# Order of the weight forms S4, S2 and the sum S3 in two up/gate pairs of an encoder step

## The chip, the cores and the metric

The kernel runs on one core of a Trainium2 chip. The metric is the device time of one execution in microseconds. The median of three runs of the kernel before is 1652.66 us (1652.25 to 1654.64).

## The reference, cut to what matters

One inference step of a one-layer encoder: two attention branches in parallel, a gated merge, and then a channel mixer, the part that matters here:

```
def conv_ffn(h, conv_buf, w_upg, conv_w, conv_b, w_down):
    u, g = jnp.split(h @ w_upg, 2, axis=-1)
    s = u.shape[1]
    upad = jnp.concatenate([conv_buf, u], axis=1)
    c = conv_b
    for tap in range(CONV_WIDTH):
        c = c + conv_w[tap] * upad[:, tap:tap + s]
    y = (jax.nn.gelu(c, approximate=True) * g) @ w_down
    return y, upad[:, -(CONV_WIDTH - 1):]
```

`h` has 1152 rows (1024 of a prompt and 8 x 16 of samples) of 1024 channels, in f32; `w_upg` is 1024 x 6144, so u and g have 3072 columns each. Everything is computed to about f32 accuracy.

## The kernel before, in words

**Products.** TensorE multiplies numbers of a shortened format (F32R), so each operand is split into a high part (a copy into F32R, on ScalarE) and a low part (the operand minus the high part, on VectorE or GpSimd). One product is three: high by high, high by low, low by high. A "form" of a weight block is this pair of high and low part, 128 x 512 each; `split` (L1108) makes it, with the copy on L1112 and the subtraction on L1113.

**Seven products instead of eight.** The up/gate stage (about 850 to 1375 us) takes the columns of u and g in 24 blocks of 128. Block f of u and block f of g make a *pair*, and the pair's weights are a 2 x 2 matrix of quarters: q[0, k] of u, q[1, k] of g, with k the half of the 1024 channels. By Winograd's form of Strassen's scheme a pair needs seven products, and each has a weight form and an activation form. In the order in which TensorE does them, with the weight form in brackets: B11 (A11), B21 (A12), B22 (S4), T2 (S2), T4 (A22), T1 of the *next* pair (S1), T3 (S3). The four A forms are quarters as they are. The others are made of sums on VectorE (tiles `s`, a pool of three buffers):

- S1 = q10 + q11 (L1105),
- S2 = S1 − q00, in place over S1 (L1127),
- S4 = q01 − S2 (L1105),
- S3 = q00 − q10 (L1105).

The last of these is the last reader of q00 and q10 in a pair, whose buffers are loaded next with the quarters of the following pair (L1100, on SP's DMA queue).

**Tokens.** The tokens are in two parts of 2 x 320 and 2 x 256 columns. Each product runs for both parts, 12 matmuls each: four channel blocks by (high, high), (high, low), (low, high), so the first two matmuls of a product need only the weight's high part, and the third needs its low part. In the trace a PSUM tile keeps the name of the product that began its sum, so the products read B11 `pa_B`, B21 `pb_B`, B22 `pc_T<-xf_B`, T2 `pa_B<-xf_T`, T4 `pb_T`, T1 `pc_T<-xf_T`, and T3 again `pa_B`, from `xfc` and `xf_T`. Each bank has two buffers, one for each part of the tokens. After a product, `after` (L1185 on) copies or adds its result into the buffers of u and g: ScalarE copies after T1, B11, B22 and T4 (L1191, L1194, L1200, L1205), VectorE adds after B21, T2 and T3 (L1197, L1203, L1207/L1208). B11 of a pair starts a new sum in the bank that T3 of the pair before used, so it needs L1208.

**Also on these engines.** After T2 the convolution of the pair (ScalarE L1228, VectorE L1230, ScalarE's GELU L1232), after T3 the gate's product on GpSimd (L1236), and during B21 the activation forms for the down projection (`z_forms`, L1258 to L1268, VectorE, and DMAs to memory on L1248/L1255). GpSimd also makes the low part of A22 (L1113).

**What sets the order.** Weight forms come out of the generator `weight_forms` in the order of TensorE's products, and the main loop asks for them some steps ahead: `fill` keeps up to three forms ahead, in four slots (`wfb`) used in turn, so a form's first write waits until the product that used its slot four forms earlier has read it. Each engine runs its instructions in one fixed order. That order is drawn up when the program is built: among the instructions that are expected to be ready, the one written first goes first, so an instruction written later overtakes one that isn't ready yet. `tc.keep_in_program_order(ins)` pins an instruction behind the one written just before it on its engine. `held_next` does so while the list `hold_next` isn't empty.

**The two places.** Pairs are numbered by their index in STEPS. Most pairs do both token parts; pairs 0 and 1 do the first part before the rest, pairs 14 and 25 do the second part of the same two blocks. In pair 2 and pair 14 the loop doesn't fill ahead as usual: after T3 (pair 2) or throughout (pair 14) it fills behind the product, and at T1 of the pair that follows (pairs 3 and 15) it doesn't fill at all. So the forms A12 and S4 of pairs 3 and 15 are made only after T3's additions, with `hold_next` set (L1402 to L1405 in the loop), and S2 is asked for at the next step, B11, with `hold_next` empty. The step after that, B21, asks for A22; B22 for S1 of the next pair.

Of the kernel before, what the change touches and what calls it, by code (L numbers as in the profile page):

```python
# [13 lines left out]
AF = mybir.ActivationFunctionType  # L14
ALU = mybir.AluOpType
# [19 lines left out]
NE = 2  # L35
# [9 lines left out]
def fr(ap):  # L45
    return ap.bitcast(F32)
# [3 lines left out]
def encoder_step(ctx, tc, x, w_in, w_o, w_out, w_upg, w_down, kc, vc, state_conv, conv_w, conv_b,  # L50
                 sink, sink_rows, t5t, onehot, relrev, g_pre_mix, g_post_mix, g_pre_ffn, g_post_ffn,
                 y, ka_new, va_new, kb_new, vb_new, conv_new):
    nc = tc.nc
# [864 lines left out]
    v, p = nc.vector, nc.gpsimd  # L918
# [122 lines left out]
    STEPS = [(f, (0,)) for f in range(NE)] + MAIN  # L1041
# [23 lines left out]
    with ExitStack() as ph:  # L1065
# [15 lines left out]
        hold_next = []  # L1081

        def held_next(ins):
            if hold_next:
                tc.keep_in_program_order(ins)
# [4 lines left out]
        def weight_forms():  # L1090

            count = 0
            pairs = {}

            def quarters(i):
                f = STEPS[i][0]
                where = {(0, 0): wqb[0][:, 0], (1, 0): wqb[0][:, 1], (0, 1): wqb[1][:, 0],
                         (1, 1): wqb[1][:, 1] if i % 2 == 0 else wq5[:]}
                for n, k in ((1, 0), (1, 1), (0, 0), (0, 1)):
                    nc.sync.dma_start(where[n, k], w_upg[n * NF + f][:, 4 * k:4 * k + 4])  # L1100
                return where

            def combine(name, a, b, op):
                t = wsp.tile([P, 4, P], F32, name=name, tag="s")
                held_next(v.tensor_tensor(t[:], a, b, op=op))  # L1105
                return t

            def split(src, eng):  # L1108
                nonlocal count
                t = wfb[count // 2 % 2][:, count % 2]  # L1110
                count += 1
                nc.scalar.activation(t[:, 0], src, AF.Copy)  # L1112
                ins = eng.tensor_tensor(t[:, 1], src, fr(t[:, 0]), op=ALU.subtract)  # L1113
                if eng is v:
                    held_next(ins)
                return t

            for i, _, names in ITEMS:
                if i not in pairs:
                    pairs[i] = (quarters(i), {})  # L1120
                q, s = pairs[i]
                for name in names:
                    if name == "S1":
                        s["12"] = combine(f"s1_{i}", q[1, 0], q[1, 1], ALU.add)
                        yield split(s["12"][:], v)
                    elif name == "S4":
                        held_next(v.tensor_tensor(s["12"][:], s["12"][:], q[0, 0], op=ALU.subtract))  # L1127
                        s["4"] = combine(f"s4_{i}", q[0, 1], s["12"][:], ALU.subtract)
                        s["3"] = combine(f"s3_{i}", q[0, 0], q[1, 0], ALU.subtract)
                        yield split(s["4"][:], v)  # L1130
                    elif name == "S2":
                        yield split(s["12"][:], v)
                    elif name == "S3":
                        yield split(s["3"][:], v)
                    else:
                        n, k = int(name[1]) - 1, int(name[2]) - 1
                        yield split(q[n, k], p if name == "A22" and i >= NE else v)
# [208 lines left out]
        dw_ahead, dz_ahead = [], []  # L1346

        forms = weight_forms()
        ahead = [next(forms) for _ in range(2)]
        rest0, rest1 = more_forms(xfp), None  # L1350
# [102 lines left out]
    with p5_stack as ph:  # L1453
        psy = ph.enter_context(tc.tile_pool(name="psy", bufs=1, space=PSUM, reuse_waits="tile"))
        q = ph.enter_context(tc.tile_pool(name="p5b", bufs=1, side="right", reuse_waits="tile"))
# [7 lines left out]
        q = more.enter_context(tc.tile_pool(name="p5c", bufs=1, side="right", reuse_waits="tile"))  # L1463
# [114 lines left out]
        for b in range(NB - 1):  # L1578
# [13 lines left out]
            if first:  # L1592

                z_forms(pr)
                t = act.tile([P, 5, 1024], F32R, name="wf5_56", tag="b0")
                zsf.append(t[:, 4].rearrange("p (a b) -> p a b", a=2))
                down["wf"] += [t[:, i:i + 2].rearrange("p i (a b) -> p i a b", a=2) for i in (0, 2)]
                t = act.tile([P, 3, 1024], F32R, name="wf5_7", tag="b1")
# [187 lines left out]
```

## Time and profile before

| | us |
|---|---|
| Median of three runs | 1652.66 |
| Profiled execution: its time | 1652.35 |
| Profiled execution: first to last instruction (span) | 1650.6 |
| TensorE matmuls busy | 1631.6 (99%) |
| VectorE busy | 1120.4 (68%) |
| ScalarE busy | 776.4 (47%) |
| GpSimd busy | 308.7 (19%) |
| Mean granted TensorE clock | 0.998 |
| One pair in the up/gate stage, TensorE | 22.3 |

In a timeline each row is the start in us, the busy time in us, the engine, the line of the kernel, the operation, what it writes and reads, the number of instructions, and in brackets the idle time of the engine ahead of it with what ended it. PE is TensorE's matmuls, PEld its weight loads, DVE VectorE, ACT ScalarE, POOL GpSimd, SP the engine that issues DMAs. Rows of the same kind that follow each other are merged. `s` are the sums, `wfb` the weight forms, `wqb` and `wq` the quarters as loaded, `wide` the buffers of u, c and g. In a row of stretches, each engine's busy time comes with its number of instructions, in the order PE, PEld, DVE, ACT, POOL.

### The profile page before, as it was taken

Reading aid. Unit: us, or ns where it says so; the run is one execution under the profiler, and the core shown is the slowest. Engines: PE = TensorE matmul, PEld = TensorE weight load, DVE = VectorE, ACT = ScalarE, POOL = GpSimd, SP = SyncE. Lnnn points to the kernel's source line nnn. Section 1 sums busy time; section 2 is a strip of 40 time slices with the busy share of each in tenths; the row PEclk is TensorE's granted clock in tenths of the full one; section 3 lists DMA queues with packets and bytes.
Section 4 is the critical chain, followed back from the end, with each engine's and each line's share of the span. In section 5 each row is a group of like instructions: output and inputs, shape, how many; then the busy total and the mean of one; then the engine's idle time right before and its main releaser. Section 6 shows DMA issues by size and latency. Waiting matters only on the chain.

```text
span 1650.6 us, 28227 instructions
## 1 busy us (share of the span) xinstructions
PE 1631.6 (99%) x10575; PEld 1496.1 (91%) x10575; DVE 1120.4 (68%) x2143; ACT 776.4 (47%) x1627; POOL 308.7 (19%) x308
## 2 busy tenths in 40 slices
PE   9999999999999999999999999999999999999997
PEld 8889889899999998988899999999999998788885
DVE  6355655565555588763488776768777779887797
ACT  5245544444444455436575444444444446433332
POOL 3000000000000000000102222332232223655404
PEclk9999999999999999999999999999999999999999
DMA  5733224232323254752222222223222248444337
GB/s 210 213 88 93 85 86 119 71 104 89 98 89 104 77 165 150 226 187 92 97 71 74 94 93 94 99 94 114 100 97 88 94 149 283 143 147 128 92 112 204
DMA packets 101272, 198.57 MB, mean 120 GB/s; under 512 B 16984, under 2 KB 32904, under 8 KB 101136
## 3 DMA queue, kind: packets, MB, share of 16 engines
q1 hardware_dynamic: 99840, 192.58, 36.7%
q0 software_dynamic: 1008, 3.67, 1.3%
q8 instruction: 83, 1.36, 0.3%
q10 hardware_dynamic: 288, 0.52, 0.1%
q14 instruction: 53, 0.43, 0.1%
HBM read 139.97 MB, written 55.70 MB: 119 GB/s over the span
## 4 chain that ended last, share of the span: by engine, by line
PE 88%; DVE 6%; issue 2%; ACT 1%; POOL 1%; DMA 1%; POOLq 0%; DVEq 0%; SPq 0%; ACTq 0%
PE pa_B L1143 12%; PE pc_T L1143 8%; PE a L1531 5%; PE pb_T L1143 4%; PE pb_B L1143 4%; PE c L1531 2%; PE r L1016 2%; PE r L1015 2%; PE r L1014 2%; PE s L1561 2%; PE o L511 2%; PE o L510 2%; PE pt L467 2%; PE s L442 1%; PE d L1531 1%
## 5 line engine op out<-in xcount | busy, mean ns | idle before, releaser
L1112 ACT ACTIVATE wfb<-s 128x512 fp32r<-128x512 f32 x96 | 60.7, 632 | 132.6 <-PE pa_B L1143 44.7
L1113 DVE TENSOR_TENSOR wfb<-s,wfb 128x512 fp32r<-128x512 f32 x96 | 80.7, 844 | 58.8 <-ACT wfb L1112 57.3
L448 ACT ACTIVATE p<-p,m 128x256 f32<-128x256 f32 (+4 forms) x128 | 76.3, 596 | 83.4 <-DVE m L444 82.1
L1143 PE MATMUL pa_B<-xf_T,wfb 128*128 128x256 f32 (+1 forms) x840 | 114.8, 289 | 0.6 <-DVE wfb L1113 0.6
L1143 PEld LDWEIGHTS pa_B<-xf_T,wfb 128*128 128x128 f32 x840 | 110.7, 188 | 0.8 <-DVE wfb L1113 0.8
L1236 POOL TENSOR_TENSOR wide<-wide 128x512 f32<-128x512 f32 (+1 forms) x46 | 80.8, 1779 | 113.8 <-DVE wide L1208 110.1
L1230 DVE SCALAR_TENSOR_TENSOR wide<-wide,cw 128x640 f32<-128x640 f32 (+2 forms) x140 | 78.9, 606 | 2.7 <-ACT wide L1228 2.6
L1143 PE MATMUL pc_T<-xf_B,wfb 128*128 128x256 f32 (+1 forms) x552 | 77.2, 294 | 1.6 <-DVE wfb L1113 1.6
L1143 PE MATMUL pc_T<-xf_T,wfb 128*128 128x256 f32 (+1 forms) x552 | 76.9, 294 | 0.1
L1143 PE MATMUL pb_T<-xf_T,wfb 128*128 128x256 f32 (+1 forms) x552 | 76.6, 294 | 0.0
L1143 PEld LDWEIGHTS pc_T<-xf_B,wfb 128*128 128x128 f32 x552 | 74.4, 188 | 2.2 <-DVE wfb L1113 2.2
L1143 PEld LDWEIGHTS pc_T<-xf_T,wfb 128*128 128x128 f32 x552 | 74.5, 188 | 0.4 <-DVE wfb L1113 0.4
L1143 PEld LDWEIGHTS pb_T<-xf_T,wfb 128*128 128x128 f32 x552 | 74.4, 188 | 0.0
L1322 POOL TENSOR_TENSOR wf<-wdB,wf 128x1024 fp32r<-128x1024 f32 x23 | 64.4, 2819 | 51.3 <-ACT wf L1321 51.3
L1228 ACT ACTIVATE wide<-wide,cb,cw 128x384 f32<-128x384 f32 (+2 forms) x70 | 46.3, 694 | 38.9 <-DVE wide L1203 38.9
L401 POOL MEMSET bt<- 64x64 f32 x16 | 2.7, 171 | 301.8 <-DMA bt<-ext_b 143.3
L1321 ACT ACTIVATE wf<-wdB 128x1024 fp32r<-128x1024 f32 x36 | 37.0, 1054 | 45.0 <-DVE wdB L1315 32.8
L1531 PE MATMUL a<-wf,z5a 128*128 128x512 f32 x240 | 57.2, 393 | 0.1
L1531 PE MATMUL a<-wf,z5b 128*128 128x512 f32 x240 | 57.0, 393 | 0.0
L1014 PE MATMUL r<-wt,ms 128*128 128x512 f32 x144 | 56.7, 393 | 0.0
L1016 PE MATMUL r<-wt,ms 128*128 128x512 f32 x144 | 56.1, 390 | 0.0
L1015 PE MATMUL r<-wt,ms 128*128 128x512 f32 x144 | 56.1, 389 | 0.0
(677 smaller groups left out, 4896.7 us busy)
## 6 DMA issues: line engine op xcount, KB each, us to landing
wqb<-in_w_upg SPq DMA_DIRECT2D x91, 256.0 KB, 2.7
zf_dr<-wide SPq DMA_DIRECT2D x84, 256.0 KB, 2.2
zr<-zf_dr SPq DMA_DIRECT2D x28, 512.0 KB, 3.8
wdB<-in_w_down SPq DMA_DIRECT2D x48, 256.0 KB, 4.1
z5a<-zf_dr SPq DMA_DIRECT2D x14, 512.0 KB, 3.6
xt<-in_x SPq DMA_DIRECT2D x9, 512.0 KB, 6.7
xr<-in_x SPq DMA_DIRECT2D x9, 512.0 KB, 3.6
x_dr<-xr SPq DMA_DIRECT2D x9, 512.0 KB, 2.6
```

The source lines that it names most:

```text
L448: nc.scalar.activation(p[:, 0:n], p[:, 0:n], AF.Exp, bias=least, scale=-1.0, accum_out=st.d[:, i:i + 1])
L1014: nc.tensor.matmul(ps[:, h], m[:, 0, k], w_rows[k][:, 0, hs], start=k == 0, stop=False)
L1015: nc.tensor.matmul(ps[:, h], m[:, 0, k], w_rows[k][:, 1, hs], start=False, stop=False)
L1016: nc.tensor.matmul(ps[:, h], m[:, 1, k], w_rows[k][:, 0, hs], start=False, stop=k == KD - 1)
L1112: nc.scalar.activation(t[:, 0], src, AF.Copy)
L1113: ins = eng.tensor_tensor(t[:, 1], src, fr(t[:, 0]), op=ALU.subtract)
L1143: nc.tensor.matmul(ps[:, 0:w], wf[:, h, k], xf[:, l, k], start=start and k == 0 and i == 0, stop=stop and k == 3 and i == 2, skip_group_ch ...
L1228: nc.scalar.activation(out, src(0), AF.Identity, bias=cb[:, f:f + 1], scale=cw[:, f, 0:1])
L1230: v.scalar_tensor_tensor(out, src(t), cw[:, f, t:t + 1], out, op0=ALU.mult, op1=ALU.add)
L1236: (v if pr.i < NE else p).tensor_tensor(c, c, pr.g[:, tokens(s)], op=ALU.mult)
L1322: ins = (v if b == 0 or b == NB - 1 or n == 8 else p).tensor_tensor(t[:, 1], src[:], fr(t[:, 0]), op=ALU.subtract)
L1531: nc.tensor.matmul(ps[:], z[:, a, k, t * P:(t + 1) * P], w[:, b, k], start=start and k == 0 and i == 0, stop=k == 1 and i == 2, skip_group ...
```

## The change

For pairs 3 and 15 (`late`: the first pair behind pair NE, and the pair behind one that does a single token part):

- the sum for S3 isn't made between the sum for S4 and S4's low part, but after S2's low part;
- S2's form is made with its ScalarE copy pinned behind the ScalarE instruction written before it (S4's copy), its low part pinned behind the VectorE instruction written before it (S4's low part), and the sum for S3 pinned behind that.

The instructions are the same, and all other pairs are written as before.

```
-            def split(src, eng):
+            def split(src, eng, pinned=False):
                 nonlocal count
                 t = wfb[count // 2 % 2][:, count % 2]
                 count += 1
-                nc.scalar.activation(t[:, 0], src, AF.Copy)
+                ins = nc.scalar.activation(t[:, 0], src, AF.Copy)
+                if pinned:
+                    tc.keep_in_program_order(ins)
                 ins = eng.tensor_tensor(t[:, 1], src, fr(t[:, 0]), op=ALU.subtract)
                 if eng is v:
                     held_next(ins)
@@
                 q, s = pairs[i]
+
+                late = i == NE + 1 or i > NE and len(STEPS[i - 1][1]) == 1
                 for name in names:
@@
                     elif name == "S4":
                         held_next(v.tensor_tensor(s["12"][:], s["12"][:], q[0, 0], op=ALU.subtract))
                         s["4"] = combine(f"s4_{i}", q[0, 1], s["12"][:], ALU.subtract)
-                        s["3"] = combine(f"s3_{i}", q[0, 0], q[1, 0], ALU.subtract)
+                        if not late:
+                            s["3"] = combine(f"s3_{i}", q[0, 0], q[1, 0], ALU.subtract)
                         yield split(s["4"][:], v)
                     elif name == "S2":
-                        yield split(s["12"][:], v)
+                        if late:
+                            hold_next.append(True)
+                        t = split(s["12"][:], v, late)
+                        if late:
+                            s["3"] = combine(f"s3_{i}", q[0, 0], q[1, 0], ALU.subtract)
+                            hold_next.pop()
+                        yield t
```

## The prediction

> **What bounds the kernel now.** I read the page first, for the span and the chain of waits.
>
> ```profile
> span 1650.6 us, 28227 instructions
> PE 88%; DVE 6%; issue 2%; ACT 1%; POOL 1%; DMA 1%; POOLq 0%; DVEq 0%; SPq 0%; ACTq 0%
> ```
>
> TensorE carries 88% of the chain, so only time in which TensorE itself stands still is worth anything. Next I asked who TensorE waited for in the up/gate stage (850 to 1370 us).
>
> ```profile
> PE pc_T L1143 <- DVE wfb L1113: 1.6, 2, 1.0
> ```
>
> Two waits, 1.6 us in all, the longer one 1.0: that is the whole prize. Then the timeline at the first place (pair 3).
>
> ```profile
> 885.36 1.51 PEld L1143 LDWEIGHTS pa_B<-xf_B,wfb 128*128 128x128 f32 x12
> ...
> 887.30 0.68 DVE L1258 TENSOR_TENSOR wide<-wide 128x512 f32<-128x512 f32 x1
> 887.48 0.63 ACT L1112 ACTIVATE wfb<-s 128x512 fp32r<-128x512 f32 x1 [1.34 <-DVE s L1127]
> 887.91 0.68 DVE L1105 TENSOR_TENSOR s<-wqb,s 128x512 f32<-128x512 f32 x1
> 888.01 0.62 ACT L1112 ACTIVATE wfb<-wq 128x512 fp32r<-128x512 f32 x1
> ...
> 888.51 0.68 DVE L1105 TENSOR_TENSOR s<-wqb 128x512 f32<-128x512 f32 x1
> ...
> 888.62 0.63 ACT L1112 ACTIVATE wfb<-s 128x512 fp32r<-128x512 f32 x1
> ...
> 888.71 1.64 POOL L1113 TENSOR_TENSOR wfb<-wq,wfb 128x512 fp32r<-128x512 f32 x1 [1.87 <-ACT wfb L1112]
> ...
> 889.11 2.38 DVE L1113 TENSOR_TENSOR wfb<-s,wfb 128x512 fp32r<-128x512 f32 x2
> ...
> 890.09 0.46 PE L1143 MATMUL pc_T<-xf_B,wfb 128*128 128x320 f32 x2
> ...
> 891.55 3.15 PE L1143 MATMUL pc_T<-xf_B,wfb 128*128 128x320 f32 x22 [1.01 <-DVE wfb L1113]
> ```
>
> ScalarE makes the high part of S2 (887.48), of A22 (888.01), then of S4 (888.62). VectorE makes the sum for S4 (887.91), the sum for S3 (888.51), then two low parts in 2.38 us. The first of the two starts at 889.11, before S4's high part has ended (889.25), so it is S2's, though the code asks for S4's form first. TensorE runs the two matmuls of B22 that need only the high part and stands still for 1.01 us until S4's low part is there (889.11 + 2.38 = 891.49). The first low part alone, from a narrower stretch of the timeline:
>
> ```profile
> 889.11 1.78 DVE L1113 TENSOR_TENSOR wfb<-s,wfb 128x512 fp32r<-128x512 f32 x1
> ```
>
> It takes 1.78 against 0.68 for the sums just ahead of it, and ends 0.54 us after GpSimd's low part of A22 (888.71 + 1.64 = 890.35; 889.11 + 1.78 = 890.89): VectorE waited for GpSimd. The sum of S3, which was already running when GpSimd began, kept its 0.68, and GpSimd then ended 1.16 us after it (889.19). The second place (pair 15), with an ordinary pair's A22 ahead of it:
>
> ```profile
> 1109.96 1.51 PEld L1143 LDWEIGHTS pa_B<-xf_B,wfb 128*128 128x128 f32 x12
> ...
> 1111.64 0.63 ACT L1112 ACTIVATE wfb<-wq 128x512 fp32r<-128x512 f32 x1 [0.91 <-PE pa_B L1143]
> ...
> 1112.36 1.29 POOL L1113 TENSOR_TENSOR wfb<-wq,wfb 128x512 fp32r<-128x512 f32 x1 [0.83 <-ACT wfb L1112]
> ...
> 1142.54 1.51 PEld L1143 LDWEIGHTS pa_B<-xf_B,wfb 128*128 128x128 f32 x12
> ...
> 1144.71 0.68 DVE L1105 TENSOR_TENSOR s<-wqb,s 128x512 f32<-128x512 f32 x1
> ...
> 1145.31 0.68 DVE L1105 TENSOR_TENSOR s<-wqb 128x512 f32<-128x512 f32 x1
> ...
> 1145.51 1.63 POOL L1113 TENSOR_TENSOR wfb<-wq,wfb 128x512 fp32r<-128x512 f32 x1 [1.87 <-ACT wfb L1112]
> ...
> 1147.27 0.46 PE L1143 MATMUL pc_T<-xf_B,wfb 128*128 128x320 f32 x2
> ...
> 1148.34 3.15 PE L1143 MATMUL pc_T<-xf_B,wfb 128*128 128x320 f32 x22 [0.62 <-DVE wfb L1113]
> ```
>
> **The change, part by part.** No instruction is added or removed. In pairs 3 and 15, S2's high part is queued behind S4's on ScalarE, S2's low part behind S4's on VectorE, and S3's sum behind both.
>
> *A22 moves up.* Its form isn't named by the change, but it stood behind S2's high part. It needs the slot of A11, free when B11's weights are loaded: in the ordinary pair it starts 0.17 us after that (1111.47 to 1111.64) and GpSimd 0.72 later. So in pair 3: 886.87 + 0.17 = 887.04, GpSimd asks at 887.76, before the sum for S4. I take it that A22 stays ahead of S4 on ScalarE, as now, since it is ready earlier.
>
> *First place.* GpSimd asks while the subtraction of L1258 runs (to 887.98), so it gets its turn then and ends 1.16 later, 889.14; the sum for S4 ends 0.54 behind it, 889.68 instead of 888.59. S4's high part starts 0.03 after the sum, as now (888.62), so at 889.71. From the start of a high part to that of its low part:
>
> ```profile
> 892.94 0.69 DVE L1105 TENSOR_TENSOR s<-wqb,wqb 128x512 f32<-128x512 f32 x1 [0.71 <-DMA wqb<-in_w_upg]
> 893.75 0.63 ACT L1112 ACTIVATE wfb<-s 128x512 fp32r<-128x512 f32 x1 [4.22 <-DVE s L1105]
> ...
> 894.41 0.69 DVE L1113 TENSOR_TENSOR wfb<-s,wfb 128x512 fp32r<-128x512 f32 x1 [0.78 <-ACT wfb L1112]
> ...
> 894.53 3.34 PE L1143 MATMUL pa_B<-xf_T,wfb 128*128 128x320 f32 x24
> ...
> 900.89 3.34 PE L1143 MATMUL pc_T<-xf_T,wfb 128*128 128x320 f32 x24
> ...
> 905.69 1.51 PEld L1143 LDWEIGHTS pa_B<-xf_T,wfb 128*128 128x128 f32 x12
> ...
> 906.41 0.48 DVE L1207 TENSOR_TENSOR wide<-wide,pa_B 128x320 f32<-128x320 f32 x1
> ...
> 907.40 1.77 PEld L1143 LDWEIGHTS pa_B<-xfa,wfb 128*128 128x128 f32 x12 [0.20 <-issue]
> ```
>
> 0.66 us. S4's low part runs from 890.37 to 891.06, and TensorE resumes 0.06 later, as now, at 891.12 instead of 891.55: 0.43 gained. Bounds: 0 if something else slips in, 1.01 if GpSimd comes after the sum (high part 888.62, low part 889.28 to 889.97, before TensorE asks).
>
> *Second place.* B11's weights are loaded at 1144.05, A22's high part starts at 1144.22, GpSimd asks at 1144.94. The sum for S4 has run since 1144.71 and keeps its 0.68, to 1145.39; GpSimd ends at 1145.39 + 1.16 = 1146.55. S4's high part starts at 1145.42, its low part is held up to 1146.55 + 0.54 = 1147.09, and TensorE wants it at 1147.73. All 0.62 is gained; bounds 0 and 0.62. Together 0.43 + 0.62 = 1.05.
>
> Of the collision, the Trainium skill (SBUF — State Buffer, section Who interferes with whom) says that VectorE instructions with two SBUF inputs and GpSimd instructions that read SBUF exclude each other, the one that starts first holding the ports for its whole instruction. The trace agrees (1.78 against 0.68); the rule speaks against the change, since A22's low part now comes earlier, against the critical sum instead of against S2's low part.
>
> *S2 comes later.* Its low part ends 0.60 behind S4's (the step from 887.91 to 888.51), at 891.66. T2 starts at 894.53 − 0.43; the rest of B22 covers it with 2.4 us, and only past that would it cost.
>
> *S3's sum comes later, and this is what gives time back.* It ends at 892.26 instead of 889.19, 3.07 later; at the second place at 1148.29 instead of 1145.99, 2.30 later. It is the last reader of two quarters, so two of the next pair's four loads move with it on SP's queue (behind them stand only loads for the pair after that; nothing moves on GpSimd's queue but A22's low part):
>
> ```profile
> wqb<-in_w_upg SPq DMA_DIRECT2D x91, 256.0 KB, 2.7
> ```
>
> The sum S1 of the next pair needs one of them. Now it starts 3.75 us after S3's sum ends (892.94 − 889.19), and VectorE is already waiting for it. Three loads were issued together then; the third no longer comes with them, so I put the step at 3.2, between the median load of 2.7 and 3.75. S1's sum then starts 2.5 us later at the first place and 1.75 at the second. T1 is safe: S1's low part would end at 895.10 + 2.5 = 897.6, against 900.46. What is queued behind S1's sum on VectorE is the next pair's other sums, T2's additions, the convolution and at last T3's addition (L1207, 906.41); 0.99 us after that one starts, B11 of the next pair gets its bank (907.40). TensorE already lost 0.20 there. The cover is VectorE's idle time in between:
>
> ```profile
> 892.94:906.41 13.47, 13.47 (x104) 13.47 (x103) 10.76 (x20) 7.93 (x17) 0.98 (x3) 1.00 0.22 69
> 1149.66:1163.07 13.41, 13.41 (x103) 13.41 (x103) 10.75 (x19) 7.96 (x17) 0.91 (x3) 1.00 0.25 71
> ```
>
> The third figure after the length is VectorE's busy time, 10.76 of 13.47 and 10.75 of 13.41, so some 2.7 us stand idle. Not all of it can be filled: 0.78 is the round trip from S1's sum over ScalarE to its low part. But T2's additions and the convolution are written ahead of the next pair's sums, so they can be queued into such gaps. I estimate that 2.4 of it is absorbed; bounds: all of it, and none. First place: 2.5 − 2.4 = 0.1 late, so pair 4's B11 starts 0.1 later than now instead of 0.43 earlier: the gain there is given back. Second place: 1.75 − 2.4 is below zero by 0.65, enough for B11 to keep the 0.62. The rows of TensorE's weight loads there:
>
> ```profile
> 1162.48 1.51 PEld L1143 LDWEIGHTS pa_B<-xf_T,wfb 128*128 128x128 f32 x12
> 1164.07 1.03 PEld L1143 LDWEIGHTS pa_B<-xfa,wfb 128*128 128x128 f32 x7
> ```
>
> B11 began within 0.08 us of T3's last load (1163.99), so this spot too has nothing to spare today.
>
> **The sum.** The profiled execution took 1652.35 us (span 1650.6); that is 0.31 below the median of the runs, 1652.66, and inside their spread (1652.25 to 1654.64). 1652.35 + 0.10 − 0.62 = 1651.83, so 1651.8.
>
> **The rivals.**
>
> *The third sum's delay gets through (slower).* VectorE runs its queue in order; if the queue still has S1's sum ahead of the convolution, it stands in front of a load that lands later, and everything up to T3's addition moves. With half of the idle time absorbed (1.35) and the step at 3.75, pair 4's B11 comes 3.07 − 1.35 = 1.72 later than now and pair 16's 2.30 − 1.35 = 0.95: 1652.35 + 2.67 = 1655.0. With nothing absorbed it is 3.07 + 2.30 = 5.37, 1657.7. With the step at 3.2 it decides the sign from 2.1 us absorbed downwards (2.5 − 2.1 + 1.75 − 2.1 is about nothing). For it: S1's sum waits for its load already now, and L1207 is already the last to arrive. Against it: 2.7 us of idle time, and work written earlier to fill it.
>
> *No collision (faster than I say).* If A22's high part ends up behind S4's on ScalarE, GpSimd begins after the sum for S4, and both waits go whole: 1.01 + 0.62 = 1.63. S3's sum is then 1.09 us earlier at the first place and nothing is given back: 1652.35 − 1.63 = 1650.7. For it: S4's form is written ahead of A22's. Against it: A22 is ready at 887.04, 0.9 us before the sum for S4 can even begin.
>
> *GpSimd first at both places (the change does nothing).* At the second place the sum for S4 leads GpSimd by 0.23 us only (1144.71, 1144.94). If GpSimd leads, it ends at 1144.94 + 1.29 = 1146.23, the sum 0.54 later at 1146.77, S4's high part starts at 1146.80, its low part ends at 1148.15, and TensorE resumes at 1148.21 instead of 1148.34: 0.13 left. S3's sum then ends at 1149.35, 3.36 instead of 2.30 later, which makes S1's sum 2.8 later and T3's addition 0.4. With the 0.1 of the first place: 1652.35 + 0.5 = 1652.9. By the rule quoted above from the Trainium skill this is settled by which of the two starts first and by nothing else.
>
> **How the numbers follow.** My forecast has a chance of 0.5, the slower rival 0.2, no collision 0.15, GpSimd first 0.15. The range begins at the case without collision, less the 0.4 by which the lowest run lies under the median: 1650.3. It ends at 1655.0, half of the idle time absorbed, and leaves out the worse half of the slower rival, about 0.1. A measurement of this kernel can tell 0.2%, 3.3 us, from no change. The whole prize is 1.63, so faster by more than that needs work to fall into another order elsewhere: 0.04. Slower by more than that needs under about 1 us absorbed at both places: 0.08. Within it: 0.88.
>
> **What would show it.** Right: TensorE no longer waits at the second place, and at the first at most 0.6; in both pairs the first low part after the sum for S4 is S4's and S3's sum comes third; GpSimd's low part of A22 starts before S4's high part, and the sum for S4 takes about 1.7 us at the first place and 0.68 at the second; the next pair's S1 sum starts 2 to 3 us later, with a longer wait for its load. Wrong: a new wait of TensorE ahead of B11 in pair 4 or 16 well over 0.3 us, a low part of S4 that still ends after 891.4 or 1148.2, or a difference in a stretch that holds neither pair.

## The result, and the profile after

The change makes the kernel slower: 1655.98 us (median of 15 runs, 1653.99 to 1659.24) against 1652.86 us for the kernel before (15 runs, 1651.46 to 1654.64). The ratio is 1.0019, with a 95% interval of 1.0012 to 1.0027. That is 3.1 us or 0.19% more: inside the 0.2% that I set as the bound for no change, though this many runs tell it apart, and 1 us beyond the upper end of my range. The profiled execution took 1654.54 us; from the page, its span:

```profile
span 1652.7 us, 28219 instructions
```

So the profiled execution is 2.2 us longer than that of before, span against span 2.1. Who TensorE waited for from 850 to 1372 us (engine, line, tile; then the total in us, the number of waits, the longest). Lines have moved: L1113 is now L1115, L1143 L1154, L1207/L1208 L1218/L1219.

```profile
PE pa_B L1154 <- DVE wide L1219: 3.2, 2, 1.7
PE pa_B L1154 <- DVE wfb L1115: 0.6, 1, 0.6
PE pc_T L1154 <- DVE wfb L1115: 0.2, 1, 0.2
PE pc_T L1154 <- ACT wfb L1112: 0.2, 1, 0.2
```

The two waits ahead of B22 have gone from 1.6 to 0.4 us. In their place stand two waits ahead of B11 of the *next* pair, 3.2 us, for T3's second addition. (The second row is a wait in T2 of the last pair, at 1370.27; it is there before the change too, at 1368.34.)

First the rows of before that the comparison needs and the prediction doesn't show: the start of B11 of pair 3, TensorE's weight load at the end of the stop in B22, S3's sum of pair 4, S1's sum of pair 5, and B11 of pair 4.

```profile
883.74 1.92 PE L1143 MATMUL pa_B<-xfa,wfb 128*128 128x320 f32 x12
...
891.55 2.94 PEld L1143 LDWEIGHTS pc_T<-xf_B,wfb 128*128 128x128 f32 x22 [1.27 <-DVE wfb L1113]
...
897.19 0.69 DVE L1105 TENSOR_TENSOR s<-wqb 128x512 f32<-128x512 f32 x1
...
905.80 0.69 DVE L1105 TENSOR_TENSOR s<-wqb,wq 128x512 f32<-128x512 f32 x1
...
907.43 2.00 PE L1143 MATMUL pa_B<-xfa,wfb 128*128 128x320 f32 x12
```

The same stretch after the change (timeline, pair 3 into pair 4). It runs 0.17 us earlier than before (B11 of pair 3 at 883.57 instead of 883.74), so 0.17 is added to its times for a comparison.

```profile
886.88 0.63 ACT L1112 ACTIVATE wfb<-wq 128x512 fp32r<-128x512 f32 x1 [0.91 <-PE pa_B L1154]
...
887.59 1.38 POOL L1115 TENSOR_TENSOR wfb<-wq,wfb 128x512 fp32r<-128x512 f32 x1 [0.92 <-ACT wfb L1112]
887.74 1.78 DVE L1105 TENSOR_TENSOR s<-wqb,s 128x512 f32<-128x512 f32 x1
...
889.55 1.15 ACT L1112 ACTIVATE wfb<-s 128x512 fp32r<-128x512 f32 x2 [2.04 <-DVE s L1105]
...
890.22 1.29 DVE L1115 TENSOR_TENSOR wfb<-s,wfb 128x512 fp32r<-128x512 f32 x2 [0.70 <-ACT wfb L1112]
...
890.96 3.14 PE L1154 MATMUL pc_T<-xf_B,wfb 128*128 128x320 f32 x22 [0.17 <-DVE wfb L1115]
891.43 0.68 DVE L1105 TENSOR_TENSOR s<-wqb 128x512 f32<-128x512 f32 x1
...
894.60 0.69 DVE L1105 TENSOR_TENSOR s<-wqb,wqb 128x512 f32<-128x512 f32 x1 [1.76 <-issue]
...
903.32 0.68 DVE L1105 TENSOR_TENSOR s<-wqb 128x512 f32<-128x512 f32 x1
...
906.81 0.69 DVE L1105 TENSOR_TENSOR s<-wqb,wq 128x512 f32<-128x512 f32 x1 [1.18 <-DMA wqb<-in_w_upg]
907.42 0.48 DVE L1218 TENSOR_TENSOR wide<-wide,pa_B 128x320 f32<-128x320 f32 x1
...
908.45 1.85 PE L1154 MATMUL pa_B<-xfa,wfb 128*128 128x320 f32 x11 [1.65 <-DVE wide L1219]
```

Read it from the top. GpSimd begins A22's low part before the sum for S4, which takes 1.78 us; S4's forms follow, then S2's, then S3's sum (891.43), then S1's sum of pair 4 (894.60). So far it goes as predicted. The new thing is lower down. S3's sum of *pair 4* stood at 897.19, ahead of the convolution; now it stands at 903.32, behind it. It is the last reader of the quarter buffers that pair 5 is loaded into. S1's sum of *pair 5* is next on VectorE, at 906.81, after a wait of 1.18 us for that load, and behind it stands T3's addition, for which TensorE waits 1.65 us.

The second place (pair 15 into pair 16; this stretch runs 1.03 us later than before):

```profile
1145.96 1.62 POOL L1115 TENSOR_TENSOR wfb<-wq,wfb 128x512 fp32r<-128x512 f32 x1 [1.31 <-ACT wfb L1112]
...
1148.29 3.34 PE L1154 MATMUL pc_T<-xf_B,wfb 128*128 128x320 f32 x24
1148.65 0.68 DVE L1105 TENSOR_TENSOR s<-wqb 128x512 f32<-128x512 f32 x1
...
1152.28 0.69 DVE L1105 TENSOR_TENSOR s<-wqb,wqb 128x512 f32<-128x512 f32 x1 [2.22 <-DMA wqb<-in_w_upg]
...
1160.94 0.67 DVE L1105 TENSOR_TENSOR s<-wqb 128x512 f32<-128x512 f32 x1
...
1164.28 0.69 DVE L1105 TENSOR_TENSOR s<-wqb,wq 128x512 f32<-128x512 f32 x1 [1.04 <-DMA wqb<-in_w_upg]
1164.89 0.48 DVE L1218 TENSOR_TENSOR wide<-wide,pa_B 128x320 f32<-128x320 f32 x1
...
1165.92 2.00 PE L1154 MATMUL pa_B<-xfa,wfb 128*128 128x320 f32 x12 [1.57 <-DVE wide L1219]
```

B22 runs through without a stop (24 matmuls in one row), and the same new wait stands ahead of B11. The chain of waits says it in order of time: start, length, what.

```profile
1161.01 0.61 DVE s L1105
1161.64 2.56 DMA wqb<-in_w_upg
...
1164.28 0.69 DVE s L1105
1164.98 0.40 DVE wide L1218
1165.37 0.41 DVE wide L1219
1165.78 0.14 issue
1165.92 2.11 PE pa_B L1154 x13
```

Late sum, load, waiting sum, T3's two additions, TensorE.

**A measure for all kernels.** I take the time from the start of B11 of the late pair to the start of B11 of the next pair. In the one kernel below in which TensorE never stops at the first place (e7) it is 905.45 − 883.21 = 22.24 us, and what is above that was lost. (At the second place e4, e7 and e9 give the same 22.24.) Before: 907.43 − 883.74 = 23.69, so 1.45 lost, and 0.94 at the second place (1164.10 less 1140.92, which is 23.18). After: 908.45 − 883.57 = 24.88, so 2.64, and 1165.92 − 1141.95 = 23.97, so 1.73. The change thus costs 1.19 + 0.79 = 1.98 us at the two places, and the down projection begins at 1374.48 instead of 1372.56, 1.92 later. The two places hold nearly the whole 2.19 by which the profiled executions differ.

### The profile page after: what moved, and what is told of

Its sections match the earlier page's. It is cut to its first block, busy times and chain, and to the rows that moved or that the text cites. A ratio compares the mean times of both kernels' runs of the same rounds, so it can differ in the third digit from the quotient of the medians.

```text
span 1652.7 us, 28219 instructions
## 1 busy us (share of the span) xinstructions
PE 1630.2 (99%) x10575; PEld 1495.4 (90%) x10575; DVE 1119.2 (68%) x2143; ACT 775.9 (47%) x1627; POOL 307.8 (19%) x308
## 3 DMA queue, kind: packets, MB, share of 16 engines
q0 software_dynamic: 1008, 3.67, 1.2%
## 5 line engine op out<-in xcount | busy, mean ns | idle before, releaser
L1115 DVE TENSOR_TENSOR wfb<-s,wfb 128x512 fp32r<-128x512 f32 x96 | 79.4, 830 | 59.2 <-ACT wfb L1112 57.5
L1154 PE MATMUL pa_B<-xf_T,wfb 128*128 128x256 f32 (+1 forms) x840 | 114.8, 289 | 0.6 <-DVE wfb L1115 0.6
L1154 PEld LDWEIGHTS pa_B<-xf_T,wfb 128*128 128x128 f32 x840 | 110.7, 188 | 0.8 <-DVE wfb L1115 0.8
L1154 PE MATMUL pc_T<-xf_B,wfb 128*128 128x256 f32 (+1 forms) x552 | 77.0, 294 | 0.3 <-DVE wfb L1115 0.2
L1154 PE MATMUL pc_T<-xf_T,wfb 128*128 128x256 f32 (+1 forms) x552 | 76.9, 294 | 0.1
L1154 PE MATMUL pb_T<-xf_T,wfb 128*128 128x256 f32 (+1 forms) x552 | 76.7, 294 | 0.0
L1154 PEld LDWEIGHTS pc_T<-xf_B,wfb 128*128 128x128 f32 x552 | 74.4, 188 | 0.8 <-DVE wfb L1115 0.4
L1154 PEld LDWEIGHTS pc_T<-xf_T,wfb 128*128 128x128 f32 x552 | 74.5, 188 | 0.4 <-DVE wfb L1115 0.4
L1154 PEld LDWEIGHTS pb_T<-xf_T,wfb 128*128 128x128 f32 x552 | 74.4, 188 | 0.0
```

The costliest lines, as they stand in the source:

```text
L1154: nc.tensor.matmul(ps[:, 0:w], wf[:, h, k], xf[:, l, k], start=start and k == 0 and i == 0, stop=stop and k == 3 and i == 2, skip_group_ch ...
```

## The experiments

Two theories, and a third that the first experiments test beside them. *The load theory*: what TensorE waits for is a quarter's load, issued late because a sum that reads its buffer last was made late; the wait is passed on because the sum that needs the load stands ahead of T3's addition in VectorE's fixed order. *The rival* (the backlog theory of the expectations): the delay of the sums itself goes down VectorE's queue, because there is too little idle time to take it up. *The swap theory*: what costs is that S4's form goes ahead of S2's, with GpSimd now in the way of S4. In the table, lost time is the measure above from the profiled execution. The difference of medians is against the runs of the kernel before that were made beside it: 1652.37 us for e1 to e4, e9 and e10, and 1651.79 for e5 to e8, which ran on another chip. So medians of the two groups are compared by their differences.

| kernel | lost, first + second place | profiled, us | median, us | difference | ratio, 95% |
|---|---|---|---|---|---|
| before | 1.45 + 0.94 | 1652.35 | 1652.86 | | |
| the change | 2.64 + 1.73 | 1654.54 | 1655.98 | +3.1 | 1.0019 (1.0012 to 1.0027) |
| e1: swap only | 1.95 + 3.27 | 1655.27 | 1654.40 | +2.0 | 1.0014 (1.0005 to 1.0023) |
| e2: sum only | 1.48 + 0.88 | 1652.78 | 1652.74 | +0.4 | 1.0003 (0.9994 to 1.0012) |
| e3: sixth buffer | 1.10 + 0.00 | 1651.48 | 1652.37 | 0.0 | 0.9999 (0.9991 to 1.0008) |
| e4: S1 behind | 0.92 + 0.00 | 1651.28 | 1651.09 | −1.3 | 0.9992 (0.9983 to 1.0000) |
| e5: S1 behind, alone | 1.26 + 0.88 | 1652.07 | 1651.72 | −0.1 | 0.9999 (0.9990 to 1.0008) |
| e6: next S3 early | 1.67 + 0.75 | 1651.92 | 1651.58 | −0.2 | 1.0000 (0.9991 to 1.0009) |
| e7: A22 on VectorE | 0.00 + 0.00 | 1650.09 | 1651.41 | −0.4 | 0.9998 (0.9989 to 1.0007) |
| e8: pair 3 only | 3.03 + 0.87 | 1652.87 | 1654.22 | +2.4 | 1.0016 (1.0007 to 1.0025) |
| e9: e4 again | 1.17 + 0.00 | 1652.03 | 1650.93 | −1.4 | 0.9993 (0.9985 to 1.0002) |
| e10: e7 again | 0.16 + 1.20 | 1651.60 | 1652.47 | +0.1 | 0.9999 (0.9990 to 1.0008) |

**e1, the swap alone.** S2's form is pinned behind S4's, but S3's sum is left where it was before the change.

```
                         s["4"] = combine(f"s4_{i}", q[0, 1], s["12"][:], ALU.subtract)
-                        if not late:
-                            s["3"] = combine(f"s3_{i}", q[0, 0], q[1, 0], ALU.subtract)
+                        s["3"] = combine(f"s3_{i}", q[0, 0], q[1, 0], ALU.subtract)
...
                         t = split(s["12"][:], v, late)
                         if late:
-                            s["3"] = combine(f"s3_{i}", q[0, 0], q[1, 0], ALU.subtract)
                             hold_next.pop()
```

> S4's form pinned ahead of S2's as in the change, but the sum for S3 left where it was, ahead of both low parts. Load theory (S3's late sum delays the next pair's sums, so the load of q10 for the pair after that lands late, and S1's sum waits for it at the head of VectorE's queue, ahead of T3's addition): TensorE's two new waits ahead of B11 (1.65 and 1.57 us) are gone, its waits ahead of B22 stay small (0.3 and 0), so about 1.3 us under the kernel before, 1651.5. Backlog theory (VectorE simply has too much in front of T3's addition after the reordering): about 1652 to 1653, with some wait left ahead of B11. Swap theory (S4 ahead of S2, with GpSimd now in its way, is what costs): as slow as the change, 1655 to 1656.

It came out slower than before by 2.0 us. That is not the gain that I expected from the load theory: putting S3's sum back is not enough. The timeline at the second place:

```profile
1145.83 1.61 POOL L1115 TENSOR_TENSOR wfb<-wq,wfb 128x512 fp32r<-128x512 f32 x1 [1.30 <-ACT wfb L1112]
1146.20 1.79 DVE L1105 TENSOR_TENSOR s<-wqb 128x512 f32<-128x512 f32 x1
...
1152.90 0.69 DVE L1105 TENSOR_TENSOR s<-wqb,wqb 128x512 f32<-128x512 f32 x1 [2.98 <-DMA wqb<-in_w_upg]
...
1166.31 0.48 DVE L1216 TENSOR_TENSOR wide<-wide,pa_B 128x320 f32<-128x320 f32 x1
...
1167.33 1.85 PE L1152 MATMUL pa_B<-xfa,wfb 128*128 128x320 f32 x11 [2.84 <-DVE wide L1217]
```

Now S3's sum is the one held up by GpSimd (1.79), and S1's sum, which needs the load that it releases, starts 4.91 us after its end (1147.99 to 1152.90), where it was 3.67 in the kernel before (1145.99 to 1149.66). Taking off the 0.90 by which this stretch runs later, S1's sum of pair 16 starts at 1152.00 instead of 1149.66, 2.34 later (1.10 from the sum, 1.24 from the longer step to the load), and T3's addition at 1165.41 instead of 1163.07: again 2.34. Nothing is absorbed, though VectorE stood idle for 2.7 us there before. Here the next pair's sums and the convolution keep the order that they have in the kernel before, and everything passes down the queue, as the rival has it. So the absorption that I counted on is a property of the order that is drawn up, and the two theories are not exclusive. The swap theory, by which e1 was to take 1655 to 1656 us, isn't far off either (1654.40 measured); e3 and e4 below decide on it.

**e2, S3's sum alone.** S2's form isn't pinned; S3's sum is made behind S2's low part.

```
                     elif name == "S2":
+                        t = split(s["12"][:], v)
                         if late:
                             hold_next.append(True)
-                        t = split(s["12"][:], v, late)
-                        if late:
                             s["3"] = combine(f"s3_{i}", q[0, 0], q[1, 0], ALU.subtract)
```

> S2's form not pinned, only the sum for S3 put behind S2's low part; S4's low part then comes third. Load theory: the sums of the next pair keep their places ahead of the convolution, so the load is late by no more than 1 to 2 us and TensorE doesn't wait ahead of B11, but S4's low part is one sum later (0.6 us) at both places: B22 waits 1.6 and 1.2 us, 1.2 us over the kernel before, 1654.1. Backlog theory: waits ahead of B11 of 1 us or more on top of that, 1656. Swap theory: no cost beyond S4's own delay, 1654.1.

Measured: no difference (+0.4 us, the interval of the ratio holds 1), and the losses are those of before, 1.48 + 0.88. I had expected S4's low part one sum later and 1.2 us more. But S3's sum stands ahead of S4's low part before the change too; here S2's low part and S3's sum have only changed places, and it is S3's sum that GpSimd holds up (1.79). From the timeline at the first place (0.24 earlier than before):

```profile
888.87 1.79 DVE L1105 TENSOR_TENSOR s<-wqb 128x512 f32<-128x512 f32 x1
...
893.92 0.69 DVE L1105 TENSOR_TENSOR s<-wqb,wqb 128x512 f32<-128x512 f32 x1 [1.93 <-issue]
...
898.31 0.68 DVE L1105 TENSOR_TENSOR s<-wqb 128x512 f32<-128x512 f32 x1
...
905.58 0.69 DVE L1105 TENSOR_TENSOR s<-wqb,wq 128x512 f32<-128x512 f32 x1
906.19 0.48 DVE L1217 TENSOR_TENSOR wide<-wide,pa_B 128x320 f32<-128x320 f32 x1
```

S3's sum ends at 888.87 + 1.79 + 0.24 = 890.90, 1.71 us later than before, where the change makes it 3.09 later. S1's sum of pair 4 starts 1.22 us later (893.92 + 0.24 = 894.16), and T3's addition at 906.43 against 906.41: this order absorbs nearly the whole delay. Pair 4's S3 sum stays ahead of the convolution (898.31), and S1's sum of pair 5 waits for nothing. An S3 sum that is late by this much is harmless alone. In the change it is costly because the next pair's S3 sum comes behind the convolution.

**e3, a sixth quarter buffer.** The change, with a buffer of its own for q10 of every second pair, so that this load no longer waits for the sum.

```
+        wq6 = wsp.tile([P, 4, P], F32, name="wq6", tag="wq6", bufs=1)
...
-                where = {(0, 0): wqb[0][:, 0], (1, 0): wqb[0][:, 1], (0, 1): wqb[1][:, 0],
+                where = {(0, 0): wqb[0][:, 0], (1, 0): wqb[0][:, 1] if i % 2 == 0 else wq6[:], (0, 1): wqb[1][:, 0],
```

> The change, with a sixth buffer for the quarters: q10 of odd pairs gets a place of its own, so that the load of q10 for the next pair no longer waits for the sum for S3. Load theory: S1's sums never wait for a load at the head of VectorE's queue, no wait ahead of B11, 1.3 us under the kernel before, 1651.5. Backlog theory: VectorE has as much in front of T3's addition as in the change; 1654 to 1656. Swap theory: 1655 to 1656.

The waits ahead of B11 for T3's addition are gone; 1.10 + 0.00 is lost, and the profiled execution is 3.1 us under that of the change. The median no longer lies 3.1 us above that of before, but only level with it. The load theory holds for the loss, and the swap theory doesn't: the order of S4 and S2 is that of the change. Why the median keeps nothing of the gain in the profile is not explained.

**e4 and e9, S1's sum behind T3's addition.** The change, with S1's sum of pairs 5 and 17 pinned behind what is written before it, so that T3's addition goes first.

```
                     if name == "S1":
+                        behind = i in (NE + 3, 17)
+                        if behind:
+                            hold_next.append(True)
                         s["12"] = combine(f"s1_{i}", q[1, 0], q[1, 1], ALU.add)
+                        if behind:
+                            hold_next.pop()
```

> The change, with S1's sum for pairs 5 and 17 pinned behind what is written before it on VectorE, so that it stands behind T3's additions of pairs 4 and 16's predecessors instead of ahead of them; the loads are as late as in the change. Load theory: the sum still has a late load, but nothing waits behind it that TensorE needs; the waits ahead of B11 are gone, 1651.5. Backlog theory: only the sum's own 0.6 us is taken out at each place, so 1 us of each wait stays, 1654.7. Swap theory: 1655 to 1656.

> e4 again, beside e10 on the same chip: 1 to 1.4 us under the kernel before by the load theory (1.6 us of waits gone ahead of B22, 0.3 left there, 0.2 to 0.3 gained ahead of B11).

Medians of 1651.09 and 1650.93 us, 1.3 and 1.4 under the kernel before, where the change is 3.1 above it; both intervals of the ratio to before reach 1.0, so a gain over before is likely but not shown. Sums and loads come as late as in the change; only the queue behind them differs. The timeline of e4 at the first place (0.25 later than before):

```profile
903.90 0.68 DVE L1105 TENSOR_TENSOR s<-wqb 128x512 f32<-128x512 f32 x1
...
906.13 0.48 DVE L1223 TENSOR_TENSOR wide<-wide,pa_B 128x320 f32<-128x320 f32 x1
...
907.15 2.00 PE L1159 MATMUL pa_B<-xfa,wfb 128*128 128x320 f32 x12
```

Pair 4's S3 sum is just as late (903.90), and B11 has no wait. What the change loses is lost because T3's addition stands behind a sum that waits for its load. The order of S4 and S2 is again that of the change, so the swap theory is out.

**e5, the pin alone.** The kernel before with the pin of e4 and nothing else of the change, to see whether the pin itself gains anything.

> The kernel before, with only the pin of e4: S1's sum for pairs 5 and 17 behind what is written before it on VectorE. Nothing of the change. Load theory (it is the late load in front of T3's addition that cost the change its gain): the pin alone frees 0.6 us of VectorE ahead of T3's addition where TensorE lost 0.20 and 0.08, so 0.2 to 0.3 us under the kernel before, not told from it; the waits ahead of B22 (1.0 and 0.6) stay. Rival (the pin is what gained in e4, not the change it was put on): 1 us or more under the kernel before.

It gains nothing (−0.1 us), and 1.26 + 0.88 is lost at the stops in B22 as before. The gain of e4 over before needs the reordering.

**e6, the next S3 sum early.** The change, with S3's sum of pairs 4 and 16 written right behind S1's form, ahead of the convolution; S1's sum of pairs 5 and 17 still ahead of T3's addition.

```
-                        yield split(s["12"][:], v)
+                        t = split(s["12"][:], v)
+                        if i in (NE + 2, 16):
+                            s["3"] = combine(f"s3_{i}", q[0, 0], q[1, 0], ALU.subtract)
+                        yield t
...
-                        if not late:
+                        if not late and "3" not in s:
```

> The change, with the sum for S3 of pairs 4 and 16 written right behind S1's form instead of behind S4's sum, so that it isn't queued behind the convolution; S1's sum for pairs 5 and 17 stays ahead of T3's addition. Load theory: the load of q10 for pairs 5 and 17 is issued about 6 us earlier, S1's sum finds it landed, the waits of 1.18 and 1.04 us on VectorE are gone and with them TensorE's waits ahead of B11: 1 us or more under the kernel before, about as e4. Rival (VectorE's amount of work between S1's sum and T3's addition is the limit, whatever it waits for): the same instructions stand ahead of T3's addition as in the change, so most of the 1.65 and 1.57 us stays and the time is 1 to 2 us over the kernel before.

```profile
895.12 0.69 DVE L1105 TENSOR_TENSOR s<-wqb 128x512 f32<-128x512 f32 x1
...
905.38 0.69 DVE L1105 TENSOR_TENSOR s<-wqb,wq 128x512 f32<-128x512 f32 x1
```

With pair 4's S3 sum at 895.12, S1's sum of pair 5 starts without a wait for its load. The loss at the two places falls from 4.37 to 2.42. The kernel is level with the one before (−0.2 us): neither the 1 us of gain that I expected from the load theory nor the 1 to 2 us of loss that the rival names. What TensorE still waits ahead of each B11 (0.68 and 0.59) is about what that sum itself takes ahead of T3's addition, 0.69; I take this for its cause, it is not shown. (The profile puts the first of these waits down to a copy on ScalarE. But T3's second addition ends at 906.86 there and B11 begins 0.15 later, as after the second addition at the second place of the change, 1165.77 to 1165.92.) What e6 does show is the other half of the load theory: the displaced S3 sum is what made the load late. The rival keeps a part: work that stands ahead of T3's addition costs time there, load or no load.

**e7 and e10, A22's low part on VectorE.** e4, with A22's low part of pairs 3 and 15 moved from GpSimd to VectorE.

```
-                        yield split(q[n, k], p if name == "A22" and i >= NE else v)
+                        yield split(q[n, k], p if name == "A22" and i >= NE and not late else v)
```

> e4, with the low part of A22 of pairs 3 and 15 on VectorE instead of GpSimd. If the sum for S4 is slow in pair 3 (1.78 us) because GpSimd holds it up, it takes 0.68 here, S4's low part is ready before TensorE asks, and the last 0.15 + 0.17 us of waiting ahead of B22 are gone: 0.3 us under e4. If it is slow for another reason, it stays at 1.78 and VectorE's extra 0.69 us makes S4's low part later: 0.4 to 0.7 us over e4.

> e7 again: with the collision with GpSimd gone too, 0.3 us under e9, 1.6 to 1.9 under the kernel before.

```profile
883.21 1.92 PE L1159 MATMUL pa_B<-xfa,wfb 128*128 128x320 f32 x12
...
887.37 0.68 DVE L1105 TENSOR_TENSOR s<-wqb,s 128x512 f32<-128x512 f32 x1
887.97 0.68 DVE L1115 TENSOR_TENSOR wfb<-wq,wfb 128x512 fp32r<-128x512 f32 x1
...
905.45 1.92 PE L1159 MATMUL pa_B<-xfa,wfb 128*128 128x320 f32 x12
```

Without GpSimd the sum for S4 takes 0.68 us instead of 1.78, and TensorE doesn't stop at either place in e7: the collision is shown. The profiled execution of e7 is 2.3 us under that of before, about what before loses (2.39). But the medians are no better than those of e4 and e9. Against the runs of before beside them e7 gains 0.4 where e4 gains 1.3, and the gain of 0.3 that I expected of e10 over e9 came out as a loss of 1.5. In the profiled execution of e10 S1's sum of pair 16 waits 3.74 us for its load (2.35 in e7), and TensorE loses 1.20 behind it:

```profile
1151.09 0.69 DVE L1105 TENSOR_TENSOR s<-wqb,wqb 128x512 f32<-128x512 f32 x1 [3.74 <-DMA wqb<-in_w_upg]
...
1163.00 2.00 PE L1159 MATMUL pa_B<-xfa,wfb 128*128 128x320 f32 x12 [1.04 <-DVE wide L1224]
```

So this load is on the path with no slack, and its time differs from one execution to the next. How often it is late was not counted.

**e8, the change at pair 3 alone.** `late = i == NE + 1`.

> The change at pair 3 alone. Load theory: at the first place 0.69 us is gained ahead of B22 and 1.65 less 0.20 is lost ahead of B11, so 0.8 us over the kernel before, with the second place as it was (a wait of 0.62 ahead of B22). A rival by which the change moves work elsewhere in the program: more than 1.5 us over the kernel before, with new waits in stretches that hold neither pair 3 nor 4.

```profile
907.05 0.69 DVE L1105 TENSOR_TENSOR s<-wqb,wq 128x512 f32<-128x512 f32 x1 [1.48 <-DMA wqb<-in_w_upg]
```

At the first place 3.03 is lost and at the second 0.87, as before (0.94): +1.5 in all, against +2.4 in the median, where I had expected 0.8. The wait of S1's sum is longer than in the first profile of the change (1.48 against 1.18), and TensorE waits 2.04 ahead of B11 instead of 1.65. From 850 to 1372 us there are no waits that the kernel before or the change doesn't have, so work moved elsewhere is not seen. The first place brings at least its share of the loss, and the second place is as it was before.

**Two more looks at the change.**

> The change itself once more, for a second profile. Load theory: the execution's time goes up and down with the waits of S1's sum in pairs 5 and 17 for its load: TensorE's waits ahead of B11 are those waits plus about 0.5 us each, and the time less them is the same in every look, about 1651.3 (1654.5 less 3.2). Rival (the spread of the change's runs comes from elsewhere, as the kernel before has one too): the waits are as in the first profile, 3.2 us in all, whatever the time.

> The change once more, for a third profile; expected as for the look before it.

Profiled at 1654.09 and 1653.97 us, with 3.09 + 1.61 and 2.84 + 1.66 lost; S1's sums of pairs 5 and 17 wait 1.29 and 1.07 in the one, 1.21 and 1.08 in the other. The waits are there in all three profiled executions. But the time doesn't follow them, as I had expected: TensorE's waits ahead of B11 add up to 3.2, 3.6 and 3.4 us in executions of 1654.54, 1654.09 and 1653.97 us, so the longest has the shortest waits. B11 of pair 16 begins at 1165.92, 1166.05 and 1166.05, so these three differ behind the two places.

## Why the prediction was wrong, by its own steps

- **The collision with GpSimd: right.** The sum for S4 was to end at 889.68, S4's high part to start at 889.71, its low part at 890.37, TensorE to resume at 891.12. With 0.17 added the rows give 889.69, 889.72, 890.39 and 891.13. The Trainium skill (SBUF — State Buffer, section Who interferes with whom) has the engine that starts first keep the ports for its whole instruction. The trace agrees: 1.78 with GpSimd first, 0.68 with that work taken off GpSimd in e7. By e1 the instruction that pays is simply the one that VectorE starts next (1.79, on S3's sum).
- **The prize: mis-sized.** I took the idle time of the matmul rows, 1.01 + 0.62 = 1.63. The stops cost more: the weight loads' idle time beside them is 1.27 (the row of before above) and 0.88, and before loses 1.45 + 0.94 = 2.39 by the measure above, the 0.20 ahead of B11 of pair 4 among it. At the second place the gain in B22 was therefore 0.88, not 0.62; at the first it was 0.42 (891.55 − 891.13), with 0.43 forecast.
- **S3's sum later: right.** 3.07 and 2.30 forecast; 891.43 + 0.68 + 0.17 = 892.28 against 889.19 is 3.09, and 1149.33 − 1.03 = 1148.30 against 1145.99 is 2.31.
- **The load and S1's sum of the next pair: nearly right.** 2.5 and 1.75 forecast; 1.83 (894.77 against 892.94) and 1.59 (1151.25 against 1149.66) measured. From the end of S3's sum to S1's sum it took 2.49 and 2.95, where I put 3.2. (The 1.75 was reckoned with the 3.75 of the first place; the rows of the second give 1149.66 − 1145.99 = 3.67 and so 2.30 + 3.2 − 3.67 = 1.83.)
- **Idle time absorbs it: right in this order, and not safe.** Without its wait, S1's sum of pair 5 would have started at 906.81 − 1.18 = 905.63, which is the 905.80 of before less 0.17. The whole 1.83 was absorbed at the first place, and at the second VectorE was even 0.25 ahead. But e1 absorbed none of its 2.34.
- **"Behind them stand only loads for the pair after that": the step that failed.** I followed the moved sum to the loads of the next pair and stopped there. To absorb the delay, the order put pair 4's S3 sum behind the convolution: 903.32 + 0.17 = 903.49 instead of 897.19, 6.3 later, and 1160.94 − 1.03 = 1159.91 instead of 1153.91, 6.0 later. S1's sum of the pair after that was already just ahead of T3's addition (905.80, then 906.41, which the prediction shows as the last to arrive), so its wait of 1.18 and 1.04 went straight to TensorE, which waited 1.65 and 1.57 ahead of B11, the first of the signs of being wrong that I had named. The absorption and the loss are the same move: what took up the idle time was work taken from in front of a sum whose load I had not followed.
- **The rival that was near.** "It stands in front of a load that lands later, and everything up to T3's addition moves" is what happened, a pair later than I placed it. I had it at 1655.0 with a chance of 0.2; the profiled executions read 1654.0 to 1654.5, and the median is 1655.98. That its number is near is partly luck: it lets half of the delay of S1's sum in pairs 4 and 16 through, and the runs show that delay absorbed and another in its place.

The sum with the measured terms: 1652.35 + 1.19 + 0.79 = 1654.33, beside 1654.54.

**What stays open.** The medians differ by 3.1, the profiled executions by 2.2 at most. The change's runs with a lower mean granted clock are the longer ones: one at 0.999 took 1654.1 us, five at 0.998 average 1654.9, six at 0.997 1656.3, three at 0.996 1657.8. Of the 33 runs of before beside e1 to e4, 12 at 0.999 average 1652.0, 18 at 0.998 1652.9, two at 0.997 1652.4, and one at 0.996 took 1654.2. At 0.998 the two stand 2.0 apart, as the profiled executions do; the two more looks, both at 0.999, lie 2.0 and 2.1 above the 1652.0 of before. In the profiled executions of before, the change, e1 and e4, taken in steps of 50 us, the clock is under 1.00 only in the first or the last step (0.94 to 0.97 there), far from the two pairs; whether the change has a hand in that, no run here tells. e3 and e7, too, gain less in the median than in the profile.

## What to carry to other kernels

When a step is moved that reads a buffer last, follow its load, the instruction that waits for that load, and what stands behind that instruction on its engine, for two rounds of the loop and not one. If an engine works in a fixed order, put what the critical engine needs ahead of anything that may wait for a load; that pin (e4) turned the change from a loss of 3 us into a likely gain of 1.3. Idle time on an engine is cover only if the order has something ready to put there, and what it puts there comes from somewhere.

## What the runs showed of the hardware

- The idle time shown at a stopped matmul is less than the stop costs: 1.01 at the matmul, 1.27 at the weight load ahead of it, and 4.44 us from B22's first matmul to T2's (890.09 to 894.53) where an undisturbed one takes 3.18 (1148.29 to 1151.47 after the change), so 1.26.
- From the end of the sum that freed a buffer to the start of the sum that needs the 256 KB load into it took 2.49 us in one place and 4.91 us in another (892.11 to 894.60 after the change, 1147.99 to 1152.90 in e1), by the same queue. In e1 three such loads were issued one behind the other; but so they were in the kernel before, where it took 3.75 and 3.67, so why e1 took longer stays open.
